# A block product's second accumulator moves from the upper half of a two-bank PSUM tile to a PSUM tile of its own

## The chip, the cores and the metric

The kernel runs on one core of one Trainium2 chip. The metric is the device time of one execution in microseconds (us). Three executions of the kernel before took 3424.34, 3412.05 and 3418.07 us; the median is 3418.07 us.

## The reference

Two layers of a decoder trunk over 1024 tokens of width 1024, all in float32. What matters for the change are the large matrix products; the attention parts are left as they are.

```python
for i in range(DEPTH):                      # DEPTH = 2
    u = rms_norm(h, attn_norm_w[i])
    proj = u @ w_in[i]                      # split into heads, gates
    fox = forgetting_attention(...)         # softmax attention with forget gates
    ret = silu(rg) * head_group_norm(chunkwise_retention(...))
    mixed = concatenate([fox, ret], -1)
    h = h + mixed @ w_out[i]
    up = rms_norm(h, ffn_norm_w[i]) @ w_up[i]        # 1024 -> 2 * 2816
    a, g = up[..., :D_FF], up[..., D_FF:]
    h = h + (gelu(causal_depthwise_conv(a, conv_w[i], conv_b[i])) * g) @ w_down[i]
    gate = sigmoid(rms_norm(h, ple_norm_w[i]) @ w_ple_gate[i])
    h = h + gate * (p[i] @ w_ple_proj[i])
return rms_norm(h, final_norm_w)
```

## The kernel before

Activations lie transposed: 128 features on the partitions, 1024 tokens along the free axis. A float32 product is made of three matmuls on operands that are split into a high and a low part (`xh,wh`, `xl,wh`, `xh,wl` in the rows). ACT makes the high part by a cast and VectorE (DVE) the low part by a subtraction.

**Block products.** Four of the products run as 2x2 block products with seven part products instead of eight: `w_out`, `w_up`, `w_down` and, in layer 0, the PLE gate. One call of `g_parts` (line 484; `parts` only runs it through) makes 256 output features for all tokens. It goes through seven parts in the order `b0 c1 b1 c2 b2 a b3` (line 310). A part is three matmuls of 128x512 for each of the `moving` operands: two of these for `w_out` and for the last group of `w_down`, three for the other groups of `w_down`, four for `w_up` and the gate, so a part has 6, 9 or 12 matmuls and a block 42, 63 or 84. The parts b0, b1, b2, b3 accumulate in one place, so that b1 adds to what b0 left there; c1 and c2 accumulate in a second place; a stands alone. After each part its sum so far is read out of PSUM ("evacuated") by `evac`: `join` (line 515, for `w_out` and `w_down`) adds it to the residual h on DVE; `form` (line 522, for `w_up` and the gate) takes b0, c1 and b1 on ACT and c2, b2, a and b3 on DVE. In all there are 96 blocks: 50 in layer 0 (8 for `w_out`, 22 for `w_up`, 16 for `w_down`, 4 for the gate) and 46 in layer 1, whose gate is done in another way.

**PSUM.** `dpsum` (line 184) gives a tile `d` of 128x1024 float32, two banks, of which there are two buffers; `spsum` (line 187) gives a tile `s` of 128x512, one bank, in four buffers. The b parts use the lower half of a `d` tile, the c parts its upper half, and part a an `s` tile. The tile framework puts the semaphores: each instruction waits for what wrote or read its tile before it, and for the release of a buffer that it takes over.

**Weights.** `Fixed` (line 411) loads a block's weights raw (`wr`), forms sums of them on POOL (`ws`), and in four stages casts them on ACT and subtracts on DVE (`w`, or `wh` and `wl`). `Line` (line 454) does this one block ahead: `line.step()` prepares one stage of the next block after parts b0, b1, b2 and b3, once the stage of the present block that used the same room is done.

**Order.** The program is scheduled by the framework, which arranges each engine's instructions by a timeline that it simulates for the program; `in_order` (line 479) ties the parts to each other on TensorE (PE) so that they keep the order in which they are written. Each engine then runs its own instructions strictly in the order in which they stand. The stages of a layer are: the input projections woven with both kinds of attention and, at their end, with the first half of `w_out` (`weave`, line 1013; the blocks at line 1085); the second half of `w_out` (1125), which also builds the operands for the next stage (`Joined`, 339); `w_up` (1148 and 1174) in pairs of blocks, the first giving `a`, to which the convolution and the gelu are applied (`conv`), the second giving `z`, which is multiplied by it and stored in DRAM (`zd`); `w_down` (1204) in four groups, whose operands are loaded (`zz`) and split again at each change of the group (`Stored`, 381); and the gate (1247).

The profile gives every instruction the line 154, a helper that records all operations, so rows are told apart by their tiles.

Of the kernel before, what the change touches and what calls it, by code (L numbers as in the profile page):

```python
# [19 lines left out]
T = 1024  # L20
# [148 lines left out]
def trunk(ctx, tc, ap):  # L169
# [11 lines left out]
    def G(name, dt=F32, shape=(P, T)):  # L181
        return arena.take(name, dt, shape)

    def dpsum():
        return ps.tile([P, T], F32, name="d", tag="d", bufs=2)

    def spsum():
        return ps.tile([P, 512], F32, name="s", tag="s", bufs=4)
# [54 lines left out]
    def weights():  # L243
        if len(ahead) < 2:
            fetch()
        return ahead.pop(0)
# [18 lines left out]
    def dense_fm(w, x):  # L265
        got = []
        for _ in g_dense_fm(w, x, got):
            pass
        return got[0]
# [209 lines left out]
    def in_order(i, before):  # L479

        tc.add_manual_dep(i.ins, before.ins.name, mybir.DependencyInfo(mybir.DependencyClass.NoSync, mybir.DependencyReason.DATA),
                          reason="order of parts")

    def g_parts(line, moving, evac, after=None):


        nonlocal behind
        w = line.take()
        d = dpsum()
        for part, name in enumerate(NAMES):  # L490
            o = spsum() if name == "a" else d[:, 512:T] if name[0] == "c" else d[:, 0:512]
            more = name in ("b1", "b2", "b3", "c2")
            for p, x in enumerate(moving):
                whi, wlo = w.of(part, p)
                xhi, xlo = x.of(part)
                first, last = p == 0 and not more, p == len(moving) - 1
                i = nc.tensor.matmul(o, whi, xhi, start=first, stop=False, skip_group_check=more)
                if p == 0 and behind is not None:
                    in_order(i, behind)
                nc.tensor.matmul(o, whi, xlo, start=False, stop=False, skip_group_check=more)  # L500
                behind = nc.tensor.matmul(o, wlo, xhi, start=False, stop=last, skip_group_check=more)
                del whi, wlo, xhi, xlo
            evac(name, o)
            if part % 2 == 0:
                w.x[part // 2] = None
                if after:
                    after(part // 2)
                line.step()
            yield 0.7 * len(moving)

    def parts(*a):
        for _ in g_parts(*a):
            pass
# [413 lines left out]
    for l in range(DEPTH):  # L927
# [143 lines left out]
        def g_out():  # L1071

            nonlocal line, u, rb
            u = rb = None
            del pr[:], ret_tab[:]
            line = Line(specs())
            for p in range(2):
                mx.append(Joined(mixed[2 * p], mixed[2 * p + 1]))
                mixed[2 * p:2 * p + 2] = [None, None]
            for q in range(4):  # L1080
                for m in (2 * q, 2 * q + 1):
                    h[m] = G("h")
                    nc.sync.dma_start(h[m], h_dram[m])
                to = h[2 * q:2 * q + 2]
                yield from g_parts(line, mx, lambda name, s: join(name, s, to))
# [5 lines left out]
        for name in ("qs", "ks"):  # L1091
            d = dense_fm(weights(), u)
# [44 lines left out]
        for j in range(FC // 2):  # L1137
# [11 lines left out]
            for i in range(2):  # L1149
                c = G("conv")  # L1150
# [9 lines left out]
            c = None  # L1160
# [6 lines left out]
            def after(n):  # L1167
                for m in u:
                    m.drop(n)
                for m in stored[0]:  # L1170
                    m.build(n)
                    if n < 3:
                        m.load(n + 1)
# [106 lines left out]
    for at, n in PIECES:  # L1280
        t = slice(at, at + n)
        pstats = Stats(n)
        for m in range(KC):
# [4 lines left out]
            d = dpsum() if m % 2 else spsum()  # L1288
# [3 lines left out]
            for i in range(parts):  # L1292
                c = slice(i * n // parts, (i + 1) * n // parts)
# [99 lines left out]
```

## Time and profile before

| | |
|---|---|
| Median of the runs | 3418.07 us (3412.05 to 3424.34) |
| Profiled execution, its own time | 3418.18 us |
| Span, first to last instruction | 3416.4 us |
| PE busy | 2829.2 us (83%), 13718 matmuls |
| DVE busy | 2025.0 us (59%) |
| ACT busy | 1226.3 us (36%) |
| POOL busy | 824.1 us (24%) |
| Mean granted clock of TensorE | 0.940 |
| DMA | 315.79 MB, 92 GB/s on average |

Busy times are shares of the whole span; a matmul's end is modelled, so that PE's pace is better read from the starts of its instructions than from its busy time. The profiled execution took 0.1 us more than the median of the runs, and 1.8 us of its own time lie outside the span.

### The profile page before, as it was taken

Reading aid. Unit: us, or ns where it says so; the run is one execution under the profiler, and the core shown is the slowest. Engines: PE = TensorE matmul, PEld = TensorE weight load, DVE = VectorE, ACT = ScalarE, POOL = GpSimd, SP = SyncE. Lnnn points to the kernel's source line nnn. Section 1 sums busy time; section 2 is a strip of 40 time slices with the busy share of each in tenths; the row PEclk is TensorE's granted clock in tenths of the full one; section 3 lists DMA queues with packets and bytes.
Section 4 is the critical chain, followed back from the end, with each engine's and each line's share of the span. In section 5 each row is a group of like instructions: output and inputs, shape, how many; then the busy total and the mean of one; then the engine's idle time right before and its main releaser. Section 6 shows DMA issues by size and latency. Waiting matters only on the chain. (4 is left out here: it accounts for less than half of the span.)

```text
span 3416.4 us, 36643 instructions
## 1 busy us (share of the span) xinstructions
PE 2829.2 (83%) x13718; PEld 2279.9 (67%) x13718; DVE 2025.0 (59%) x3031; ACT 1226.3 (36%) x1820; POOL 824.1 (24%) x652
## 2 busy tenths in 40 slices
PE   9998997668888877776689989976788888777778
PEld 8887885456666655554478878964566666555557
DVE  4565565665665665556545655556665655755457
ACT  4454433333333332223334535232333332422133
POOL 2222322222222222212322223322222222222121
PEclk9999998879999999998899999988799999999999
DMA  4223214122222252222233232141222222442114
GB/s 152 80 76 95 65 48 136 52 68 93 99 86 84 90 207 96 86 66 92 105 106 87 69 94 73 41 139 43 80 75 93 93 98 94 157 138 90 56 62 133
DMA packets 116866, 315.79 MB, mean 92 GB/s; under 512 B 13520, under 2 KB 34512, under 8 KB 116688
## 3 DMA queue, kind: packets, MB, share of 16 engines
q1 hardware_dynamic: 113616, 305.05, 27.7%
q10 hardware_dynamic: 3072, 8.39, 1.0%
q8 instruction: 108, 1.77, 0.2%
q14 instruction: 70, 0.57, 0.1%
HBM read 210.04 MB, written 69.80 MB: 82 GB/s over the span
## 5 line engine op out<-in xcount | busy, mean ns | idle before, releaser
L154 PE MATMUL d<-xh,wh 128*128 128x512 f32 x1560 | 684.2, 439 | 461.6 <-DVE h L154 264.4
L154 PEld LDWEIGHTS d<-xh,wh 128*128 128x128 f32 x1560 | 309.4, 198 | 684.0 <-DVE h L154 173.2
L154 PE MATMUL d<-xl,wh 128*128 128x512 f32 x1560 | 641.4, 411 | 6.7 <-DVE xl L154 6.7
L154 PE MATMUL d<-xh,wl 128*128 128x512 f32 x1560 | 641.5, 411 | 0.0
L154 POOL TENSOR_TENSOR ws<-ws,wr 128x512 f32<-128x512 f32 (+2 forms) x192 | 228.0, 1187 | 930.9 <-DMA zd<-t 330.2
L154 POOL TENSOR_TENSOR ws<-wr 128x512 f32<-128x512 f32 (+2 forms) x192 | 253.2, 1320 | 696.7 <-DVE wl L154 253.8
L154 ACT CAST wh<-ws 128x1024 fp32r<-128x1024 f32 (+2 forms) x192 | 170.7, 889 | 635.7 <-PE d L154 487.0
L154 DVE TENSOR_TENSOR h<-h,d 128x512 f32<-128x512 f32 x288 | 196.9, 684 | 305.6 <-PE d L154 305.2
L154 PEld LDWEIGHTS d<-xh,wl 128*128 128x128 f32 x1560 | 311.6, 200 | 72.4
L154 PEld LDWEIGHTS d<-xl,wh 128*128 128x128 f32 x1560 | 312.8, 200 | 60.9 <-DVE xl L154 7.8
L154 DVE TENSOR_TENSOR wl<-ws,wh 128x1024 fp32r<-128x1024 f32 (+2 forms) x192 | 206.6, 1076 | 241.9 <-ACT wh L154 234.9
L154 PE MATMUL d<-dh,uh 128*128 128x256 f32 (+1 forms) x768 | 224.5, 293 | 17.5 <-DVE flog L154 10.3
L154 PE MATMUL d<-x,w 128*128 128x512 f32 x936 | 229.5, 390 | 6.6 <-DVE x L154 5.1
L154 PE MATMUL d<-dl,uh 128*128 128x256 f32 (+1 forms) x768 | 223.3, 291 | 3.7 <-POOL dl L154 3.7
L154 PE MATMUL d<-dh,ul 128*128 128x256 f32 (+1 forms) x768 | 222.0, 290 | 0.0
L154 PE MATMUL d<-uh,dh 128*128 128x512 f32 (+1 forms) x584 | 193.1, 399 | 28.5 <-ACT dh L154 24.8
L154 PEld LDWEIGHTS d<-x,w 128*128 128x128 f32 x936 | 175.4, 188 | 44.4 <-DVE x L154 6.3
L154 POOL TENSOR_TENSOR dl<-dr,dh 128x1024 fp32r<-128x1024 f32 (+2 forms) x51 | 123.8, 2429 | 307.7 <-PE d L154 131.0
L154 PE MATMUL d<-ul,dh 128*128 128x512 f32 (+1 forms) x584 | 191.4, 395 | 1.9 <-DVE ul L154 1.8
L154 PE MATMUL d<-uh,dl 128*128 128x512 f32 (+1 forms) x584 | 189.4, 391 | 1.9 <-DVE dl L154 1.4
L154 PEld LDWEIGHTS d<-dh,uh 128*128 128x128 f32 x768 | 150.6, 196 | 21.4 <-DVE flog L154 10.7
L154 PEld LDWEIGHTS d<-dl,uh 128*128 128x128 f32 x768 | 150.9, 197 | 5.7 <-POOL dl L154 4.7
(209 smaller groups left out, 5323.2 us busy)
## 6 DMA issues: line engine op xcount, KB each, us to landing
wr<-in_wup_dram SPq DMA_DIRECT2D x88, 512.0 KB, 3.6
zz<-zd SPq DMA_DIRECT2D x66, 512.0 KB, 4.2
wr<-in_wdown_dram SPq DMA_DIRECT2D x48, 384.0 KB, 3.6
zd<-z SPq DMA_DIRECT2D x66, 256.0 KB, 2.0
dr<-in_wqk_dram SPq DMA_DIRECT2D x32, 512.0 KB, 3.5
hs<-h SPq DMA_DIRECT2D x24, 512.0 KB, 3.0
h<-hs SPq DMA_DIRECT2D x24, 512.0 KB, 6.0
zd<-t SPq DMA_DIRECT2D x22, 512.0 KB, 4.3
```

What stands on the lines that cost most here:

```text
L154: ins = f(*[bare(v) for v in a], **{n: bare(v) for n, v in k.items()})
```

## The change

The tile `d` now serves the b parts alone; its upper half stays unused. The c parts get an `s` tile, taken at c1 and used again at c2. Part a takes an `s` tile of its own, as before. Nothing else is edited, and the engines have the same instructions in number and kind.

```diff
@@ -486,9 +486,13 @@
 
         nonlocal behind
         w = line.take()
-        d = dpsum()
+        b, c = dpsum()[:, 0:512], None
         for part, name in enumerate(NAMES):
-            o = spsum() if name == "a" else d[:, 512:T] if name[0] == "c" else d[:, 0:512]
+            if name in ("c1", "a"):
+                o = spsum()
+                c = o if name == "c1" else c
+            else:
+                o = c if name == "c2" else b
             more = name in ("b1", "b2", "b3", "c2")
             for p, x in enumerate(moving):
                 whi, wlo = w.of(part, p)
```

On PE the parts stand as they stood. Here is the end of part b0 and the start of part c1 in a `z` block of `w_up` in layer 0, before; the names carry the buffer's number, and the bracket names the engines or queues whose semaphores the instruction waits for:

```order
L154 MATMUL d_7896<-x_6016,w_7776 128x512 x3
L154 MATMUL d_7896<-x_6126,w_7776 128x512 x3
L154 MATMUL d_7896<-x_6236,w_7776 128x512 x3
L154 MATMUL d_7896<-x_6346,w_7776 128x512 x3
L154 MATMUL d_7896<-xh_6019,wh_7808 128x512 [waits Activation_49]
L154 MATMUL d_7896<-xl_6020,wh_7808 128x512
```

And the same place now:

```order
L154 MATMUL d_7915<-x_6021,w_7794 128x512 x3
L154 MATMUL d_7915<-x_6132,w_7794 128x512 x3
L154 MATMUL d_7915<-x_6243,w_7794 128x512 x3
L154 MATMUL d_7915<-x_6354,w_7794 128x512 x3
L154 MATMUL s_7932<-xh_6024,wh_7827 128x512 [waits Activation_49]
L154 MATMUL s_7932<-xl_6025,wh_7827 128x512
```

Part c1 writes another tile than b0. It still waits for an ACT instruction, since its weights `wh` are cast there. A part later, where c1 ends and b1 starts, the row of PE now reads:

```order
L154 MATMUL s_7932<-xh_6357,wh_7827 128x512
L154 MATMUL s_7932<-xl_6358,wh_7827 128x512
L154 MATMUL s_7932<-xh_6357,wl_7828 128x512
L154 MATMUL d_7915<-xh_6024,wh_7827 128x512 [waits Activation_49]
L154 MATMUL d_7915<-xl_6025,wh_7827 128x512
```

Here b1 returns to the tile of b0 and waits for ACT, which evacuates b0. Elsewhere PE's rows have moved only where `w_out` is woven with the attention, in the attention of layer 1, and around the gate.

The scheduler has also moved a few instructions of other engines. On DVE, in the `z` blocks of `w_up`, this stood before (`conv` is the convolution's result, `wl` the next block's low weights, the last row the evacuation of c2):

```order
L154 TENSOR_TENSOR conv_7610<-conv_7610,rb_6506 128x1024 [waits Activation_49]
L154 SCALAR_TENSOR_TENSOR conv_7616<-a_7489,convp_177,conv_7616 128x1022 [waits DVE_49]
L154 TENSOR_TENSOR conv_7616<-conv_7616,rb_6506 128x1024 [waits Activation_49]
L154 TENSOR_TENSOR wl_7675<-ws_7671,wh_7674 128x1024 [waits PE_49,Activation_49]
L154 TENSOR_TENSOR z_7622<-z_7622,d_7628 128x512 [waits DMAHW6_49,DMAHW4_49,PE_49]
```

And this stands there now:

```order
L154 TENSOR_TENSOR conv_7627<-conv_7627,rb_6515 128x1024 [waits Activation_49]
L154 SCALAR_TENSOR_TENSOR conv_7633<-a_7505,convp_177,conv_7633 128x1022 [waits DVE_49]
L154 TENSOR_TENSOR wl_7693<-ws_7689,wh_7692 128x1024 [waits PE_49,Activation_49]
L154 TENSOR_TENSOR conv_7633<-conv_7633,rb_6515 128x1024 [waits Activation_49]
L154 TENSOR_TENSOR z_7639<-z_7639,s_7662 128x512 [waits DMAHW6_49,DMAHW4_49,PE_49]
```

The low weights and the last product with `conv` have changed places. On ACT at the same place the order before was, from the first gelu on:

```order
L154 ACTIVATE conv_7610<-conv_7610 128x1024 [waits DVE_49,Activation_49]
L154 ACTIVATE z_7623<-d_7628 128x512 [waits PE_49]
L154 ACTIVATE conv_7616<-conv_7616 128x1024 [waits DVE_49,Activation_49]
L154 COPY z_7622<-d_7628 128x512 [waits PE_49]
L154 CAST wh_7674<-ws_7671 128x1024 [waits Pool_49]
```

And it is now:

```order
L154 ACTIVATE conv_7627<-conv_7627 128x1024 [waits DVE_49,Activation_49]
L154 ACTIVATE z_7640<-s_7662 128x512 [waits PE_49]
L154 COPY z_7639<-d_7645 128x512 [waits PE_49]
L154 CAST wh_7692<-ws_7689 128x1024 [waits Pool_49]
L154 ACTIVATE conv_7633<-conv_7633 128x1024 [waits DVE_49,Activation_49]
```

The evacuation of b1 (the COPY) and the cast of the next weights have moved ahead of the second gelu.

## Rows read from the trace of the kernel before

**Rows 1.** The page: the span, and the busy time of the engines (PEld is PE's weight load).

```profile
span 3416.4 us, 36643 instructions
...
PE 2829.2 (83%) x13718; PEld 2279.9 (67%) x13718; DVE 2025.0 (59%) x3031; ACT 1226.3 (36%) x1820; POOL 824.1 (24%) x652
```

**Rows 2.** Busy time by stretch. The columns are the stretch and its length in us; the busy us, with the number of instructions, of PE, of its weight loads, of DVE, ACT and POOL; TensorE's granted clock; the DMA engines' busy share; GB/s. The rows are, in layer 0, the four woven blocks of `w_out`, the four others, the first two blocks of `w_up`, its other twenty, the twelve `w_down` blocks with three operands, the four with two, and the gate.

```profile
559.20:631.00 71.80, 53.30 (x218) 39.82 (x218) 45.33 (x78) 16.52 (x30) 17.13 (x20) 0.90 0.14 43
631.00:721.30 90.30, 57.99 (x170) 39.80 (x169) 62.01 (x86) 34.12 (x48) 18.56 (x16) 0.72 0.19 68
721.30:789.00 67.70, 49.05 (x201) 37.72 (x200) 40.86 (x42) 22.48 (x28) 18.86 (x12) 0.87 0.20 67
789.00:1251.30 462.30, 404.62 (x1682) 309.16 (x1681) 283.90 (x309) 157.55 (x189) 105.83 (x77) 1.00 0.29 96
1251.30:1511.70 260.40, 196.00 (x758) 145.35 (x757) 141.79 (x173) 67.14 (x84) 59.12 (x52) 0.93 0.34 116
1511.70:1595.20 83.50, 50.46 (x169) 34.93 (x168) 59.85 (x80) 32.03 (x45) 21.22 (x19) 0.84 0.22 73
1595.20:1741.80 146.60, 100.69 (x405) 77.33 (x403) 76.19 (x68) 47.12 (x57) 31.67 (x16) 0.86 0.30 106
```

**Rows 3.** The same view for layer 1, the twenty regular blocks of `w_up` and the twelve of `w_down`, and, in the last row, a stretch of the attention of layer 0.

```profile
2512.40:2974.60 462.20, 404.63 (x1681) 309.15 (x1680) 282.89 (x309) 157.95 (x190) 106.73 (x77) 1.00 0.29 96
2974.60:3235.90 261.30, 195.90 (x758) 145.39 (x758) 141.61 (x173) 67.08 (x84) 56.83 (x50) 0.93 0.34 116
...
400.00:500.00 100.00, 100.00 (x644) 90.40 (x644) 57.56 (x92) 28.71 (x41) 32.73 (x17) 1.00 0.22 57
```

**Rows 4.** All waits of PE in the twenty regular blocks of `w_up` of layer 0: who waited for whom, us in total, times, longest us.

```profile
PE d L154 <- ACT a L154: 21.0, 30, 0.9
PE d L154 <- ACT z L154: 20.8, 30, 0.7
PE d L154 <- DVE z L154: 8.0, 10, 1.0
PE d L154 <- DVE a L154: 7.8, 10, 0.8
```

**Rows 5.** PE in order of time in one `z` block of `w_up`: start, length, what, and in brackets the idle time ahead of it and what ended it. The rows are part b0, the first matmuls of c1 and of b2, and part b0 of the next block.

```profile
904.49 2.88 PE L154 MATMUL d<-x,w 128*128 128x512 f32 x12
908.10 0.50 PE L154 MATMUL d<-xh,wh 128*128 128x512 f32 x1 [0.72 <-ACT z L154]
...
919.28 0.50 PE L154 MATMUL d<-xh,wh 128*128 128x512 f32 x1 [0.78 <-DVE z L154]
...
927.57 2.88 PE L154 MATMUL d<-x,w 128*128 128x512 f32 x12
```

**Rows 6.** ACT in order of time in the same block: the evacuation of b0, the second gelu, the evacuation of b1, and the cast of the next weights.

```profile
907.46 0.59 ACT L154 COPY z<-d 128x512 f32<-128x512 f32 x1 [0.17 <-ACT conv L154]
...
913.12 1.06 ACT L154 ACTIVATE conv<-conv 128x1024 f32<-128x1024 f32 x1 [1.38 <-DVE conv L154]
914.85 0.58 ACT L154 COPY z<-d 128x512 f32<-128x512 f32 x1 [0.66 <-PE d L154]
915.33 1.05 ACT L154 CAST wh<-ws 128x1024 fp32r<-128x1024 f32 x1
```

**Rows 7.** DVE in order of time in the same block: the evacuation of part a of the block before, the convolution's last step, its last product, the low weights, the evacuation of c2.

```profile
901.97 0.69 DVE L154 TENSOR_TENSOR a<-a,s 128x512 f32<-128x512 f32 x1 [0.17 <-PE s L154]
...
911.75 1.28 DVE L154 SCALAR_TENSOR_TENSOR conv<-a,convp,conv 128x1022 f32<-128x1022 f32 x1
914.22 1.42 DVE L154 TENSOR_TENSOR conv<-conv,rb 128x1024 f32<-128x1024 f32 x1 [1.19 <-ACT conv L154]
916.41 1.47 DVE L154 TENSOR_TENSOR wl<-ws,wh 128x1024 fp32r<-128x1024 f32 x1 [0.77 <-ACT wh L154]
918.54 0.69 DVE L154 TENSOR_TENSOR z<-z,d 128x512 f32<-128x512 f32 x1 [0.66 <-PE d L154]
```

**Rows 8.** PE in `w_down`: b0 of a regular block, the first matmul of its c1, the start of the next block; then b0 and the first matmul of c1 in the first block after a change of the group; and, in the last two rows, the sums of PE's waits over the twelve blocks with three operands and over the four with two.

```profile
1283.95 2.20 PE L154 MATMUL d<-x,w 128*128 128x512 f32 x9
1287.03 0.47 PE L154 MATMUL d<-xh,wh 128*128 128x512 f32 x1 [0.87 <-DVE h L154]
...
1302.69 0.62 PE L154 MATMUL d<-x,w 128*128 128x512 f32 x2
...
1342.22 2.20 PE L154 MATMUL d<-x,w 128*128 128x512 f32 x9
1349.85 0.77 PE L154 MATMUL d<-xh,wh 128*128 128x512 f32 x1 [5.43 <-DVE h L154]
...
PE d L154 <- DVE h L154: 64.4, 48, 11.4
...
PE d L154 <- DVE h L154: 33.0, 17, 8.4
```

**Rows 9.** DVE at that change of the group: two splits of new operands and the evacuation of b0 behind them.

```profile
1342.16 3.68 DVE L154 TENSOR_TENSOR xl<-zz,xh 128x1024 fp32r<-128x1024 f32 x2
...
1349.03 0.67 DVE L154 TENSOR_TENSOR h<-h,d 128x512 f32<-128x512 f32 x1
```

**Rows 10.** The sums of PE's waits for evacuations over the second four blocks of `w_out` of layer 0, and over the gate.

```profile
PE d L154 <- DVE h L154: 27.7, 15, 7.1
...
PE d L154 <- ACT sg L154: 37.9, 11, 12.6
```

## The prediction

> **What bounds the kernel now.** I first read the page's busy times [rows 1]: TensorE (PE) is busy for 83% of the span, no other engine for more than 59%, so PE or something that PE waits for sets the time. The table by stage [rows 2] then shows where PE is not full. The stages made of block products take 559.2 to 1741.8 us in layer 0, and PE is busy for some 75% or less of each of them but the regular part of `w_up`, where it is 404.62 of 462.30 us. The attention, by contrast, has a stretch of 100 us in which PE never stops [rows 3].
>
> What PE waits for is plainest in `w_up`, since all twenty blocks are alike: its waits are 80, four to each block, half of them on ACT's and the rest on both engines' evacuations, each 0.7 to 0.8 us [rows 4]. In order of time [rows 5]: part b0 starts at 904.49 with twelve matmuls. The pace of matmuls is (2.88 - 2.20) / 3 = 0.2267 us, from a run of twelve [rows 5] and one of nine [rows 8]. So b0 has been issued at 907.21. ACT evacuates it from 907.46 to 908.05 [rows 6], and c1 starts at 908.10, 0.05 us later. But c1 writes the other half of the tile, which nobody is reading: it waits because both halves are one tile. The same happens at b1, c2 and b2, but not at part a, which has a tile of its own, nor at b3, which follows a and whose tile was evacuated meanwhile. Four waits per block, 96 blocks: that is the path that the change touches.
>
> **The change, part by part.** It moves c1 and c2 to another tile. No instruction is added. Then c1 need not wait for b0's evacuation, b1 waits for that of b0 only after c1 has run, and so on: each evacuation gets one part's time as cover, 6, 9 or 12 matmuls, which is 1.36, 2.04 or 2.72 us, against some 0.9 us from b0's last issue to c1's start [rows 5]. Where an evacuation comes later than that cover, only the cover is gained.
>
> *Regular `w_up` blocks.* A block takes 927.57 - 904.49 = 23.08 us [rows 5]; its 84 matmuls need 84 x 0.2267 = 19.04. The difference is 4.04 us, four waits of 1.01: 0.89 of standing still and the slow first matmuls after it. Forty such blocks, 162 us. The two stage rows agree: 462.3 - 20 x 19.04 = 81.5 us a layer [rows 2, 3].
>
> The other engines must keep up with 19 us. DVE has 283.90 us of work in the twenty blocks [rows 2], 75% of 381 us. The moved instructions need a look, for DVE and ACT stand in order. In a `z` block, with part a of the block before evacuated from 901.97 on [rows 7] as zero, the convolution's last step ends at 11.1. This chain does not wait for c1, so it stays. Then b1 of the `z` block will end at about 10.7 (b3, b0, c1 and b1 after part a, at 2.72 each). Its COPY on ACT, 0.58, ends at 11.5, the cast of `wh`, 1.05, at 12.5 [rows 6], the low weights, at most 1.47, at 14.0, the last product, 1.42, at 15.4 and the evacuation of c2, 0.69, at 16.1 [rows 7]. Part b2 ends at 16.1, is evacuated by 17.0, and b3 needs that at 18.9. So 1.9 us are to spare, and I cost the moves at nothing. If POOL's sums or a crowded DVE take more than that, each pair of blocks loses the excess; one us would make 20 us in all.
>
> *The first two `w_up` blocks of each layer* take 67.7 us [rows 2] against 38.1 of matmuls; most of the rest is woven-in work and operands that are late. I take the regular share, 8 a layer: 16 us.
>
> *`w_down` with three operands.* A regular block takes 1302.69 - 1283.95 = 18.74 us [rows 8] against 63 x 0.2267 = 14.28: 4.46 to gain, for twelve blocks 53.5. At a change of the group it is otherwise. There b0 is issued by 1344.26, but its evacuation stands on DVE behind splits of the next operands until 1349.03 [rows 9], and c1 waits until 1349.85 [rows 8]. Afterwards c1 fills 2.04 us of that and b1 waits for the rest. Three changes a layer give some 1 us more each than a regular wait; but the splits do not get shorter, and a little of what the blocks before them gain is waited for here. I take 55 a layer, 110 us. The bounds are 2 x 45, if the changes of group swallow 10, and 2 x 64, the waits that the trace counts [rows 8].
>
> *Blocks with two operands*, sixteen of `w_out` and eight of `w_down`. The four waits are worth 4.04 at the regular price and at most 4 x 1.36 plus slow starts, 5.9. DVE is the nearest bound here: 62.01 of 90.30 us in the second half of `w_out` [rows 2]; with 17 us gone it is at 85%. The waits there are 27.7 us in 15 times [rows 10], two a time as long as the regular one, so part of them stays. I take 4.2 a block, 100 us; between 2.5 and 5.9 a block that is 60 to 142.
>
> *The gate*, four blocks, with 37.9 us of waits in 11 times [rows 10], the longest 12.6. The long ones come at c1, behind ACT's queue, and give one part, 2.72; three regular ones give 3.0. Less in the last block: 21 us.
>
> *The clock.* It is 1.00 in regular `w_up` and 0.72 to 0.93 in the stages with long idle times [rows 2]. Half of the idle time goes, so some of the time at 1.2 GHz should too; but the longest idle times, those at changes of group, are only cut by a part. The bounds are nothing and, if all of it went, some 90 us a layer at most (one minus the clock, times the length, over the rows), less where PE stands still anyway. I take 10 us, near nothing, because what stays idle is what the low clock follows.
>
> The sum: 162 + 16 + 110 + 100 + 21 + 10 = 419 us. The profiled execution's own time is 3418.18 us, 1.8 over its span and 0.1 over the median of the runs. 3418 - 419 = 2999 us.
>
> **The rivals.**
>
> *DVE takes over.* The cover of a part is 1.36 us in the small blocks; an evacuation of about 0.9 with a weight subtraction of 0.7 to 1 us ahead of it on DVE is longer. If half of each wait stays in the 48 blocks of two and three operands, 48 x 4 x 0.5 = 96 us are lost again: 3095 us. For it: 62 of 90 us [rows 2]. Against it: DVE itself idles 0.66 to 1.19 us ahead of its instructions in the regular stage [rows 7]. Chance 0.12.
>
> *PSUM gets scarce.* The c tile holds one of four `s` buffers for three parts, beside a's, and where `w_out` is woven with the retention both want them. If the eight woven blocks gain nothing and lose as much, that is 2 x 8 x 4.2 = 67 us: 3066. Against it: outside the weaving only c and a want the ring, two a block, so that a buffer comes round after two blocks. Chance 0.03. The Trainium skill (Perfetto Trace Analysis, Matmul Optimizations) advises to put all eight PSUM banks to use, and the change leaves the upper halves of two tiles empty, so it speaks against the change; its section Matmuls, on turning evacuations and matmul groups over different banks, speaks for it, and [rows 5] side with the latter.
>
> *It does not do what it says.* c1 still waits for ACT after the change, for its weights; were that the wait that binds, the time would stay at 3418. Against it: c1 starts 0.05 us after b0's evacuation [rows 5, 6], and c2 and b2 wait for evacuations likewise [rows 4]. Chance 0.02.
>
> *Slower: the clock falls in the denser stretches.* The 96 blocks hold 48 x 19.04 + 24 x 14.28 + 24 x 9.52 = 1485 us of matmuls. Each us of them at 1.2 GHz costs another, so the gain is gone once 28% of them run there, and at 40% the time is 3009 + 594 = 3603 us. Against it: the clock is 1.00 where PE is busy without a break, and 1.00 in 462 us with four idle times per block [rows 2, 3]. Chance 0.02. The Trainium skill (TensorE: Matmul & The Clock Gate, A second HAM failure mode: psum-queue depth-cycling) tells of a kernel whose clock swung because PE idled briefly between matmul groups that cycle through PSUM banks; the trace here shows such short idle times at full clock.
>
> **How the numbers follow.** The forecast, 2999, has a chance of 0.81. Its bounds: the two-operand blocks at 60 instead of 100 and `w_down` at 90 instead of 110 make 3059; the same terms at 142 and 128 and 15 us more of the clock make 2924. The range from 2940 to 3090 takes in most of this and almost the first rival. About 0.3%, 10 us, is what a measurement of this kernel can tell from no change. Faster: 0.81 + 0.12 + 0.03 = 0.96; the same: 0.02; slower: 0.02.
>
> **What the profile after would show.** Right: a `w_up` block every 19 to 19.5 us; PE's waits on `a`, `z` and on evacuations of regular blocks gone; the remaining waits at b1 after a change of the group; ACT and DVE busy times as before, in a shorter span. Wrong: waits of PE that reappear at b1, c2, b2 or b3 with DVE full; a `w_up` pair above 39 us; a granted clock below 1.00 in `w_up`; or c1 still behind the evacuation of b0.

## The result, and the profile after

The changed kernel takes 2996.9 us (median; 2995.72 to 2997.99) against 3421.2 us of the kernel before measured beside it: 0.8761 of its time, 95% interval 0.8739 to 0.8784. The forecast was 2999 us. The profiled execution took 2996.09 us with a span of 2994.2 us, 422.2 less than before [rows 1]; its mean granted clock is 0.956, before 0.940.

The page of the kernel after, span and busy times:

```profile
span 2994.2 us, 36622 instructions
...
PE 2706.9 (90%) x13718; PEld 2278.8 (76%) x13718; DVE 2069.8 (69%) x3031; ACT 1216.1 (41%) x1820; POOL 877.9 (29%) x652
```

The same number of instructions on PE, DVE, ACT and POOL, in a span that is an eighth shorter. PE's busy time fell by 122 us, so it is not the waits alone that went: the slow first matmuls behind each wait (0.50 us in [rows 5]) went with them, and fewer matmuls run at the lower clock. DVE's and POOL's busy times rose by 45 and 54 us, although their counts are those of [rows 1].

Busy time by stretch of the kernel after; the columns and the first seven stages are those of [rows 2], the last two are the regular `w_up` and `w_down` of layer 1, as in [rows 3]:

```profile
558.70:612.50 53.80, 47.76 (x224) 38.17 (x224) 43.26 (x78) 16.71 (x30) 18.76 (x20) 0.97 0.19 61
612.50:678.10 65.60, 46.63 (x170) 34.08 (x170) 59.47 (x86) 31.43 (x47) 14.62 (x13) 0.90 0.25 88
678.10:740.70 62.60, 47.74 (x201) 38.20 (x200) 41.44 (x43) 24.62 (x30) 26.00 (x14) 0.84 0.23 80
740.70:1127.00 386.30, 383.27 (x1682) 314.77 (x1682) 309.03 (x306) 151.85 (x187) 123.64 (x77) 1.00 0.34 114
1127.00:1329.60 202.60, 180.72 (x758) 146.64 (x757) 143.58 (x175) 69.24 (x86) 60.47 (x52) 0.95 0.45 152
1329.60:1394.20 64.60, 44.90 (x170) 33.66 (x169) 60.46 (x79) 31.58 (x45) 25.49 (x19) 0.92 0.27 92
1394.20:1520.50 126.30, 98.12 (x401) 78.85 (x400) 77.11 (x70) 48.43 (x57) 31.80 (x16) 0.85 0.37 125
...
2242.80:2631.00 388.20, 383.36 (x1681) 314.68 (x1681) 307.80 (x307) 153.41 (x190) 123.48 (x77) 1.00 0.35 114
2631.00:2834.00 203.00, 182.49 (x757) 147.14 (x756) 143.21 (x176) 67.52 (x84) 57.16 (x50) 0.94 0.45 151
```

Each length subtracted from that of before gives the gain of a stage. By the terms of the forecast, both layers together:

| Term | Forecast, us | Measured, us | From |
|---|---|---|---|
| regular `w_up`, 40 blocks | 162 | 150.0 | 76.0 + 74.0 |
| first two `w_up` blocks | 16 | 11.4 | 5.1 + 6.3 |
| `w_down`, three operands | 110 | 116.1 | 57.8 + 58.3 |
| two operands, 24 blocks | 100 | 122.4 | 18.0 + 24.7 + 18.9, and 16.3 + 22.2 + 22.3 |
| gate | 21 | 20.3 | 146.6 - 126.3 |
| clock | 10 | inside the terms above | |
| the rest of the span | 0 | 2.0 | what is left of 422.2 |

PE's waits by releaser (us in total, times, longest), in the order regular `w_up` of layer 0 and of layer 1, the second four `w_out` blocks, `w_down` with three operands (two rows) and with two, the gate:

```profile
PE s L154 <- ACT a L154: 2.9, 7, 0.7
...
PE s L154 <- ACT a L154: 4.8, 8, 2.1
...
PE d L154 <- DVE h L154: 12.1, 8, 3.2
...
PE d L154 <- DVE h L154: 18.1, 6, 7.1
PE s L154 <- DVE h L154: 3.7, 1, 3.7
...
PE d L154 <- DVE h L154: 19.7, 8, 5.0
...
PE d L154 <- ACT sg L154: 23.4, 3, 9.9
```

Of the 80 waits in a layer's regular `w_up` [rows 4] seven or eight are left, and they are of another kind (below). In `w_down` 48 waits became 7 [rows 8], in the second half of `w_out` 15 became 8, and in the gate 11 became 3 [rows 10]: the short regular ones are gone, the long ones behind queued work remain.

PE in order of time, after: part b0 of a `z` block and of the `a` block behind it, and c2 of the latter; then, at a change of the group in `w_down`, b3 of the last block and b1 of the first; and c2 of an `a` block of layer 1:

```profile
836.82 2.88 PE L154 MATMUL d<-x,w 128*128 128x512 f32 x12
...
855.86 2.88 PE L154 MATMUL d<-x,w 128*128 128x512 f32 x12
...
864.57 0.50 PE L154 MATMUL s<-xh,wh 128*128 128x512 f32 x1 [0.39 <-ACT a L154]
...
1199.78 0.50 PE L154 MATMUL d<-xh,wh 128*128 128x512 f32 x1 [2.06 <-DVE h L154]
...
1209.58 0.80 PE L154 MATMUL d<-xh,wh 128*128 128x512 f32 x1 [3.38 <-DVE h L154]
...
2330.32 0.50 PE L154 MATMUL s<-xh,wh 128*128 128x512 f32 x1 [2.08 <-ACT a L154]
```

The `z` block takes 855.86 - 836.82 = 19.04 us, to the hundredth the 84 x 0.2267 us of its matmuls; before, it took 23.08 [rows 5].

### The profile page after: what moved, and what is told of

Read it like the earlier page. It is cut to its first block, busy times and chain, and to the rows that moved or that the text cites. A ratio compares the mean times of both kernels' runs of the same rounds, so it can differ in the third digit from the quotient of the medians.

```text
span 2994.2 us, 36622 instructions
## 1 busy us (share of the span) xinstructions
PE 2706.9 (90%) x13718; PEld 2278.8 (76%) x13718; DVE 2069.8 (69%) x3031; ACT 1216.1 (41%) x1820; POOL 877.9 (29%) x652
## 5 line engine op out<-in xcount | busy, mean ns | idle before, releaser
L154 PE MATMUL d<-xh,wh 128*128 128x512 f32 x936 | 384.4, 411 | 112.4 <-DVE h L154 88.8
L154 PE MATMUL s<-xh,wh 128*128 128x512 f32 x936 | 378.6, 404 | 51.7 <-ACT wh L154 12.7
L154 PE MATMUL s<-xh,wl 128*128 128x512 f32 x936 | 373.0, 398 | 11.0 <-DVE wl L154 11.0
L154 PE MATMUL s<-xl,wh 128*128 128x512 f32 x936 | 373.7, 399 | 4.4 <-DVE xl L154 4.4
L154 PE MATMUL d<-xl,wh 128*128 128x512 f32 x936 | 376.4, 402 | 0.0
L154 PE MATMUL d<-xh,wl 128*128 128x512 f32 x936 | 376.3, 402 | 0.0
L154 PEld LDWEIGHTS s<-xh,wh 128*128 128x128 f32 x936 | 181.4, 194 | 104.2 <-ACT wh L154 15.6
L154 PEld LDWEIGHTS s<-xh,wl 128*128 128x128 f32 x936 | 181.0, 193 | 51.9 <-DVE wl L154 13.3
L154 PEld LDWEIGHTS s<-xl,wh 128*128 128x128 f32 x936 | 181.7, 194 | 42.9 <-DVE xl L154 5.8
L154 PEld LDWEIGHTS d<-xl,wh 128*128 128x128 f32 x936 | 183.2, 196 | 36.7
```

What stands on the lines that cost most here:

```text
L154: ins = f(*[bare(v) for v in a], **{n: bare(v) for n, v in k.items()})
```

## The experiments

The theory: a wait is put on the whole tile, and each evacuation now has one part's time as cover. The rivals: it is the buffers in PSUM that count, in which pool and how many; or something else that the new tiles brought along, such as the order of the moved instructions or the clock.

**The change in `w_up` alone.** Only blocks with four operands get a tile of their own for c; the others keep both halves of one `d` tile.

```diff
-        b, c = dpsum()[:, 0:512], None
+        d = dpsum()
+        wide = len(moving) == 4
+        b, c = d[:, 0:512], None if wide else d[:, 512:T]
...
-            if name in ("c1", "a"):
+            if name == "a" or name == "c1" and wide:
...
-                o = c if name == "c2" else b
+                o = c if name[0] == "c" else b
```

> The c parts get a tile of their own only in the blocks with four operands (w_up and the gate); in w_out and w_down they lie in the upper half of d as before. If the time comes from the waits at c1, b1, c2 and b2 for a tile that is shared, stage by stage, then the change's gain in w_up and the gate comes alone: 150 + 11 + 20 = 181 us as measured in the changed kernel's stages, so 3421 - 181 = 3240 us, give or take 15; a regular w_up block takes 19.0 to 19.7 us and a regular w_down block with three operands still 18.7. If the gain came from the order that the scheduler now finds, or from the clock over the whole run, it is not divided in this way and the time is anywhere else, under 3200 or over 3300.

Measured: 3227.93 us (3225.93 to 3229.76) against 3411.56, ratio 0.9454 (0.9432 to 0.9476). The regular `w_up` and the three-operand `w_down` of its layer 0, and PE's waits in that `w_down`:

```profile
783.80:1168.90 385.10, 383.16 (x1681) 314.70 (x1680) 309.58 (x307) 153.51 (x189) 122.68 (x77) 1.00 0.34 115
1168.90:1428.30 259.40, 195.94 (x758) 145.18 (x757) 144.27 (x175) 67.33 (x85) 57.34 (x52) 0.93 0.35 119
```

```profile
PE d L154 <- DVE h L154: 63.5, 48, 8.3
```

`w_up` has all of its gain, `w_down` none: its 48 waits are those of [rows 8]. So the gain comes block by block from the tile, and 184 of some 420 us belong to four-operand blocks.

**The second tile from the other pool.** c takes the lower half of a `d` tile instead of an `s` tile, so other banks, and both `d` buffers serve one block.

```diff
-                o = spsum()
+                o = spsum() if name == "a" else dpsum()[:, 0:512]
```

> The c parts take the lower half of a second two-bank tile d instead of an s tile, so that s is left to part a and the attention, and b and c of successive blocks share two buffers. If a tile of its own with one part's time as cover is all that counts, the time is that of the changed kernel, 2997 us, give or take 10: the next block's c1 takes the buffer of b and waits for b3's evacuation, which part b0 covers. If the gain needs buffers that are free a whole block ahead, each block waits once more for about 1 us, 96 in all, so 3094 us. If the c tiles made the s ring scarce in the woven blocks, these get faster by some us each and the time is under 2985.

Measured: 2998.43 us (2994.95 to 2999.91), ratio 0.8781 (0.8763 to 0.8798). Its woven `w_out` blocks and regular `w_up` of layer 0:

```profile
556.70:609.00 52.30, 47.23 (x218) 37.52 (x218) 42.45 (x75) 16.28 (x30) 18.76 (x20) 0.97 0.20 62
737.60:1124.40 386.80, 383.62 (x1682) 314.45 (x1681) 309.56 (x306) 152.23 (x188) 123.14 (x77) 1.00 0.34 114
```

No different from the changed kernel: 0.8781 and 0.8761 of the time before, with intervals that overlap. So neither the pool of the second tile nor the fact that both buffers of `d` serve one block counts; it is enough that c and b are two tiles. The upper halves of `d` stay empty in both kernels, so which banks stay empty was not varied here.

**Every evacuation by ACT done twice, after and before.** In `form`, the evacuations of b0, c1 and b1 by ACT are written a second time: the same values, 0.58 us more each. In one run in the changed kernel, in another in the kernel before.

```diff
-            nc.scalar.copy(c11 if name == "b0" else c12, s)
+            for _ in range(2):
+                nc.scalar.copy(c11 if name == "b0" else c12, s)
...
-            nc.scalar.activation(c22, s, AF.Copy, scale=-1.0)
+            for _ in range(2):
+                nc.scalar.activation(c22, s, AF.Copy, scale=-1.0)
```

After:

> The changed kernel with each evacuation that ACT makes in w_up and the gate (b0, c1, b1) done twice, so that each takes 0.57 us more. If a part's time covers them now, 2.72 us against 0.9 + 0.57, it costs next to nothing: 2997 to 3010 us, and the regular w_up blocks stay at 19.0 to 19.8 us. If evacuations were still on PE's path, 48 x 3 x 0.57 = 82 us are added: 3079.

Measured: 3001.4 us (2998.76 to 3001.71), ratio 0.8789 (0.8772 to 0.8806). Regular `w_up` of layer 0:

```profile
739.40:1127.10 387.70, 383.19 (x1681) 314.70 (x1680) 305.44 (x307) 184.69 (x249) 123.29 (x77) 1.00 0.34 114
```

ACT has 33 us more to do here (184.69 against 151.85), and the stage is 1.4 us longer. Evacuations of twice the length stay within the cover.

Before:

> The kernel before with the same doubled evacuations. If PE stands still from the end of a part to the end of its evacuation, all of the added time shows: 48 x 3 x 0.57 = 82 us, so 3503 us, give or take 15, and a w_up block takes 23.1 + 1.7 = 24.8 us. If the wait at c1, b1 and c2 is for something else (weights, operands), the time stays near 3421.

Measured: 3605.29 us (3600.86 to 3611.65), ratio 1.0561 (1.0537 to 1.0585). The direction is that of the theory, the size is not: 194 us instead of 82. Nineteen of the regular `w_up` blocks of layer 0, then PE and ACT in order of time in an `a` block:

```profile
797.30:1316.00 518.70, 405.33 (x1598) 308.49 (x1597) 258.29 (x287) 171.26 (x230) 104.97 (x76) 0.96 0.24 79
```

```profile
1019.48 0.50 PE L154 MATMUL d<-xh,wh 128*128 128x512 f32 x1 [1.68 <-ACT a L154]
...
1028.93 0.50 PE L154 MATMUL d<-xh,wh 128*128 128x512 f32 x1 [2.11 <-ACT a L154]
...
1029.83 0.63 PE L154 MATMUL d<-xh,wh 128*128 128x512 f32 x1
1030.26 0.63 PE L154 MATMUL d<-xl,wh 128*128 128x512 f32 x1
```

```profile
1026.86 0.58 ACT L154 COPY a<-d 128x512 f32<-128x512 f32 x1 [3.11 <-PE d L154]
1027.34 1.05 ACT L154 CAST wh<-ws 128x1024 fp32r<-128x1024 f32 x1
1028.29 0.59 ACT L154 COPY a<-d 128x512 f32<-128x512 f32 x1
```

A block takes 518.70 / 19 = 27.3 us instead of 23.1. The forecast had priced the second copy alone, at 0.57 us a piece. But the scheduler put the cast of the next weights, 1.05 us, between the two copies of b1, so c2 waits 2.11 us instead of some 0.7; c1, whose evacuation of b0 has a cast of 0.62 between its copies, waits 1.68. And the clock no longer stays at 1.00: behind the wait of 2.11 us, matmuls start 0.43 us apart for some 3 us, 1.2 GHz, and the stage's mean is 0.96. So the pair says: before, ACT's queue is on the path at each evacuation, after, it is not; how much of the 194 us is the second copy as such, the pair does not say. An estimate from the rows: three copies of 0.58 us are 1.7 of the 4.2 us that a block lost, some 84 us in 48 blocks; the casts that came onto the path and the lower clock would be the rest.

**A repeat of the changed kernel**, as a mark for the runs beside it.

> The changed kernel once more, to be compared with the two below on the same chip: 2997 us, give or take 5.

Measured: 2996.08 us (2992.3 to 2999.91), ratio 0.8751 (0.8735 to 0.8767).

**Other rooms for the parts of an `a` block.** What is left in regular `w_up` is c2 of the `a` blocks. ACT in order of time in the kernel after: c1's evacuation in that `a` block, and one in layer 1:

```profile
863.92 0.60 ACT L154 ACTIVATE a<-s 128x512 f32<-128x512 f32 x1 [4.03 <-DMA zd<-t]
...
2329.67 0.60 ACT L154 ACTIVATE a<-s 128x512 f32<-128x512 f32 x1 [1.99 <-DMA zd<-t]
```

In the first, c1 has been issued at 855.86 + 24 x 0.2267 = 861.30. ACT starts its evacuation at 863.92, and what it waited for is not PE but a store to DRAM: the room in SBUF that it writes is one from which the stored sums `t` still leave. In this run the rooms are taken before the stores of the `z` block are made, so that the two don't share one.

```diff
-            body = [G("a") for i in range(2)]
+            body, spare = spare or [G("a") for i in range(2)], None
...
             act = body = None
+            spare = None if last else [G("a") for i in range(2)]
             store_stages(*z, zd[j])
```

> The changed kernel, with the rooms of the next pair's a tiles taken before those of the stored sums t. In the changed kernel the evacuation of c1 in the a blocks of w_up waits until the store of t has landed, since it writes into that room, and c2 stands still for 0.3 to 0.8 us. If that is what keeps the regular w_up stage at 386 and 388 us a layer instead of 381, the time falls by 8 to 13 us, to 2984 to 2989, and all twenty blocks take 19.05 us. If it is DVE, slowed where POOL runs at the same time, or the next weights, the time stays at 2997.

Measured: 2985.28 us (2982.7 to 2990.83), ratio 0.8723 (0.8708 to 0.8738), 10.8 us under the repeat of the changed kernel beside it. Regular `w_up` of both layers:

```profile
742.20:1123.00 380.80, 380.80 (x1682) 315.31 (x1681) 293.64 (x306) 154.90 (x188) 120.16 (x77) 1.00 0.35 116
...
2240.50:2621.30 380.80, 380.80 (x1681) 315.31 (x1680) 294.25 (x306) 154.95 (x188) 121.03 (x77) 1.00 0.36 115
```

PE is busy for the whole 380.80 us, which is 20 x 19.04: the forecast's bound, in both layers. So what regular `w_up` fell short by was this store's. DVE's busy time fell as well, from 309.03 to 293.64 us, but none of PE's waits in this stage of the kernel after was for DVE.

**ACT evacuates first.** Where DVE joins b0, b1 and b2 to `h`, and stands behind splits, ACT first copies the part into a scratch tile in SBUF, which sets the tile in PSUM free; DVE adds the copy.

```diff
     def join(name, s, to):
...
+            if name in ("b0", "b1", "b2"):
+                out = hb("out")
+                nc.scalar.copy(out, s)
+                s = out
             nc.vector.tensor_tensor(dst, dst, s, op=op)
```

> The changed kernel, but in w_out and w_down ACT first copies b0, b1 and b2 out of PSUM, and DVE adds the copies to h. The waits that are left there are for DVE, 12.1 us in the second half of w_out, 18.1 in w_down with three operands and 19.7 with two in layer 0. If they come from evacuations that stand behind splits in DVE's queue while the operands are ready, PE's waits fall by half or more and the time by 25 to 50 us, to 2947 to 2972. If the operands themselves are late (DVE's work as such is the bound there), or ACT's queue holds the copies just as long, the time stays within 10 us of 2997 or rises.

Measured: 3021.7 us (3018.97 to 3027.26), ratio 0.8828 (0.8812 to 0.8844): 26 us slower than the repeat beside it. The second half of `w_out`, the three-operand and the two-operand `w_down` of layer 0; then PE and ACT in that `w_out`:

```profile
613.10:686.20 73.10, 46.82 (x170) 34.28 (x169) 61.55 (x90) 37.42 (x59) 15.21 (x13) 0.84 0.23 77
1137.90:1334.10 196.20, 177.95 (x758) 144.13 (x757) 144.90 (x174) 85.80 (x123) 58.97 (x52) 0.96 0.49 166
1334.10:1408.10 74.00, 46.88 (x170) 36.25 (x169) 60.61 (x79) 36.32 (x55) 21.85 (x20) 0.79 0.22 76
```

```profile
649.32 0.80 PE L154 MATMUL d<-xh,wh 128*128 128x512 f32 x1 [9.65 <-ACT out L154]
```

```profile
645.75 1.06 ACT L154 ACTIVATE hsq<-h 128x1024 f32<-128x1024 f32 x1 [0.47 <-DVE xl L154]
648.69 0.58 ACT L154 COPY out<-d 128x512 f32<-128x512 f32 x1 [1.88 <-DVE ssq L154]
```

With three operands the stage is 6.4 us shorter than after the change (202.60), with two it is 7.5 and 9.4 us longer. There the copy stands on ACT behind `hsq`, which had waited 0.47 us for DVE, and then waits 1.88 us more for DVE itself, until `ssq` has ended: the evacuation is late by two queues instead of one, and PE idles 9.65 us. What the copy needs of `ssq` the row does not say; the scratch tile takes a room in SBUF too, but no run tried another one.

**Both, the copy only where it helped**: the rooms of the run before last, and ACT's copy only in `w_down` blocks with three operands; beside it the rooms alone once more.

```diff
-    def join(name, s, to):
+    def join(name, s, to, first=False):
...
+            if first and name in ("b0", "b1", "b2"):
+                out = hb("out")
+                nc.scalar.copy(out, s)
+                s = out
...
-                parts(line, mx, lambda name, s: join(name, s, to), after if q == 3 else None)
+                parts(line, mx, lambda name, s: join(name, s, to, len(mx) == 3), after if q == 3 else None)
```

> The rooms taken in the other order, and ACT copying b0, b1 and b2 out of PSUM first, but only in the twelve w_down blocks of a layer that have three operands, whose queue on ACT is short. In the run with the copies in all of w_out and w_down these twelve blocks took 196 and 199 us, against 203 in the changed kernel, mostly because b3 no longer waited 2.2 us for DVE in the last block of a group, while w_out and the rest of w_down lost 8 to 10 us a stage to ACT's queue. If that reading is right, this version gains 8 to 12 us on the one above, a ratio of about 0.869. If the copies cost ACT or DVE as much elsewhere (the evacuations that stay on DVE come later), it is no faster.

> The kernel with the rooms taken in another order, once more beside the one below: a ratio of 0.872 to before, give or take 0.002.

Measured: 2978.09 us (2968.85 to 2981.43), ratio 0.8707 (0.869 to 0.8725), and for the rooms alone 2985.07 us (2984.95 to 2986.78), ratio 0.8737 (0.8725 to 0.875). The intervals just touch, so the copy's gain of some 7 us is likely and no more; it is a little less than the 8 to 12 us expected. Its stage in layer 0:

```profile
1121.50:1317.80 196.30, 178.04 (x758) 144.02 (x757) 143.93 (x174) 86.81 (x123) 58.53 (x52) 0.96 0.49 166
```

Against 203.80 us with the rooms alone that is 7.5 us in this layer. By the starts of the blocks it is 6.0 in the other, and part of it is lost again, most in the stretch of gate and attention (671.0 against 666.4 us). This version is the fastest of all that ran, and faster than both kernels.

## Why the prediction was right

**The sum: closer than its terms.** The span fell by 422.2 us where the terms made 419. Regular `w_up` and its first two blocks came out 16.6 us under the forecast, `w_down` with three operands and the two-operand blocks with the clock 18.5 over it, the gate 0.7 under, and the rest of the span gave 2.0. The mechanism held; that the errors cancel to 3 us is luck.

**The tile, not the bank.** Right: a block goes at the pace of its matmuls once b and c are two tiles, and whose tiles they are makes no difference (the run with c in the other pool). That rules out the rival of scarce PSUM: the woven blocks gained 18.0 and 16.3 us instead of losing any, and they take 52.30 us without `s` buffers for c against 53.80 with them in the two profiles, so these cost some 1.5 at most. The advice of the Trainium skill to use all eight banks (Perfetto Trace Analysis, Matmul Optimizations) was no guide here: the kernel before used both halves of each `d` and the four `s` buffers, and the faster one leaves two upper halves empty. What its section Matmuls says of turning evacuations and matmul groups over different banks held, with the addition that the framework must see them as different tiles.

**Regular `w_up`: 150 instead of 162.** This term was sized too high. The four waits of 1.01 us per block went as forecast (of the 80 a layer, 60 were for ACT and 20 for DVE [rows 4], so three quarters for ACT and not half). What the step left out is who else holds an evacuation back: I had followed engines and queues, not the SBUF room that the evacuation writes. With the waits on PSUM gone, ACT reaches c1's evacuation in the `a` blocks before the store from that room has landed, and c2 waits, mostly 0.2 to 0.7 us and once 2.08. By the starts of the blocks, three of the twenty pairs took more than the 39 us that the prediction named as a sign of being wrong: 39.05, 39.06 and 40.48 us. The run with other rooms gives this back: 386.30 + 388.20 - 2 x 380.80 = 12.9 us in the two stages, 10.8 in the whole. The first two blocks of a layer gave 11.4 of 16 us: three long waits stay there in layer 0, 4.3 to 5.4 us, two of them for weights, which the forecast had left out.

**The `z` block's chain: no loss, but less spare than I said.** DVE in order of time in the kernel after: low weights, the last product, the evacuations of c2 and b2, and low weights of the same size a little later; then, in `w_down`, two splits of new operands with the evacuation of b2 behind them, and the evacuation of b0 in the next block:

```profile
846.75 2.21 DVE L154 TENSOR_TENSOR wl<-ws,wh 128x1024 fp32r<-128x1024 f32 x1 [0.39 <-ACT wh L154]
848.88 2.30 DVE L154 TENSOR_TENSOR conv<-conv,rb 128x1024 f32<-128x1024 f32 x1
851.11 0.67 DVE L154 TENSOR_TENSOR z<-z,s 128x512 f32<-128x512 f32 x1
851.71 0.67 DVE L154 TENSOR_TENSOR z<-z,d 128x512 f32<-128x512 f32 x1
...
859.64 1.22 DVE L154 TENSOR_TENSOR wl<-wr,wh 128x1024 fp32r<-128x1024 f32 x1
...
1195.45 3.67 DVE L154 TENSOR_TENSOR xl<-zz,xh 128x1024 fp32r<-128x1024 f32 x2
1199.05 0.67 DVE L154 TENSOR_TENSOR h<-h,d 128x512 f32<-128x512 f32 x1
...
1208.85 0.67 DVE L154 TENSOR_TENSOR h<-h,d 128x512 f32<-128x512 f32 x1
```

b2 is evacuated by 852.38; b3 is due at 836.82 + 72 x 0.2267 = 853.14. That leaves 0.8 us where I had 1.9, since the low weights and the product take 2.21 and 2.30 us instead of 1.47 and 1.42 [rows 7]. The cover held, but with less than half of the margin that the forecast counted on.

**`w_down` with three operands: 116 for 110.** The waits behind splits stayed, as forecast, and the one at the change moved from c1 to b1, where it is 3.38 us instead of 5.43 [rows 8]: cut by one part's time, 2.04. Not foreseen: in the last block of a group b3 waits too, 2.06 us, since b2's evacuation stands behind 3.67 us of splits on DVE. Of `w_up` I had written that b3 does not wait, because part a comes between; here its 2.04 us are not enough. The new order has a part in this: at that place of the kernel before, one split, 1.22 us from 1337.82 on, stood between the evacuations of c2 and b2, and now there are two, with POOL's sums beside them. A wait of 2.04 to 2.06 us at b3 comes at the end of two groups in each layer. The sum is nevertheless a little above the forecast; the clock's rise from 0.93 to 0.95 is in it.

**Two operands and the clock: 122 for 100 and 10.** The waits were about right, the clock was not. Where 1.2 GHz is granted, matmuls start 0.43 us apart instead of 0.2267, so each loses 0.20 us. In the stages of the 96 blocks 445 matmuls start in such stretches before and 276 after, which is 89 and 55 us: 34 instead of my 10. In those of the two-operand blocks it is 50 and 21. The rows show it in the second half of `w_out`: clock 0.72 before, 0.90 after, and PE's busy time fell by 11.4 us for the same 170 matmuls, the slow first ones behind a wait included. Without these 29 us the two-operand blocks gained some 93, near the forecast. I had argued that what stays idle is what the low clock follows; but here the idle time that went was itself much of it. That the clock rose because the short waits went was not tried by a run of its own, and a slow stretch that hides in a wait would make the 29 an upper bound.

**The gate, and the other rivals.** 20.3 us for 21. DVE did not take over: it is busy for 59.47 of 65.60 us in the second half of `w_out`, 91% where I had 85, and waits of 12.1 us on it remain there, but the stage gained 24.7 us, where that rival left it 4 x (4.2 - 2.0) = 8.8. A change without effect and a clock that falls in denser stretches are refuted by the rows of `w_up` (386.30 us, clock 1.00). The Trainium skill's page on the clock (TensorE: Matmul & The Clock Gate, A second HAM failure mode: psum-queue depth-cycling) tells of short idle times between groups that cost the clock: with waits of 0.7 to 0.8 us this kernel kept 1.00 [rows 2, 4], with three of 1.3 to 2.1 us in an `a` block it fell to 0.96 (the kernel before with its evacuations doubled). So the trace shows such a loss there, and this change moved away from it.

**The order of the moved instructions.** Not tried: the new tile with the order of before, since the scheduler moves instructions with it in every run. For regular `w_up` the traces still tell the two apart. What moved there on ACT and DVE stands in the `z` blocks; in the `a` blocks ACT, DVE and POOL have the same sequence before and after. In the kernel before, the `a` block ahead of the `z` block of [rows 5] starts here:

```profile
881.39 2.88 PE L154 MATMUL d<-x,w 128*128 128x512 f32 x12
```

It takes 904.49 - 881.39 = 23.10 us. After, the `a` blocks of this layer take 19.04 to 20.02 us, with other rooms all of them 19.04. So there the gain came without the moves. In `w_down` the new order has a part in the wait at b3 above; what it costs or gives by itself, there and in the other stages, stays open.

## What to carry to other kernels

A wait that ends 0.05 us after the evacuation of *another half* of a tile is a wait for nothing: give each accumulator that is written and read at its own times a tile of its own, even if banks stay empty, where the framework sets its waits by tile as here. Price the gain as the smaller of the exposed evacuation and the time of the part that runs in between, and then look along the evacuation for what it needs besides its engine, the room that it writes included. Moving evacuations to a second engine helps only where that engine's queue is not itself waiting for the first.

## What the hardware showed that was not expected

Instructions of DVE and POOL that run side by side take longer here than alone. POOL in order of time in the `z` block of the kernel after, three sums of weights:

```profile
846.58 1.29 POOL L154 TENSOR_TENSOR ws<-ws,wr 128x512 f32<-128x512 f32 x1 [12.22 <-DVE conv L154]
847.84 4.51 POOL L154 TENSOR_TENSOR ws<-wr 128x512 f32<-128x512 f32 x2
```

One such sum takes 1.29 us when it comes first, and 4.51 / 2 = 2.26 in the two after it. DVE's subtraction and product over 128x1024 beside them take 2.21 and 2.30 us; the subtraction at 859.64, with POOL idle, takes 1.22. The times fit a strict alternation: the subtraction begins at 846.75 and ends at 848.96, 1.09 after POOL's first sum (847.87); the two evacuations on DVE, which read one operand from PSUM, take their 0.67 us while POOL is still at work. The Trainium skill (SBUF — State Buffer, Who interferes with whom) says that a DVE instruction with two inputs in SBUF and a POOL instruction that reads SBUF contend for a port that is locked and not divided, and that a DVE instruction with at most one SBUF input, outside its 2-port modes, does not contend. The trace agrees with both halves; the prediction had named POOL's sums and a crowded DVE and priced them at nothing.

Its price depends on the order of the work. Over regular `w_up`, DVE is busy for 309.03 us with 306 instructions where it had 283.90 with 309 [rows 2]; with other rooms it is 293.64 with 306, and POOL's time is 120.16 instead of 123.64. No run varied this overlap alone.
